# Stick-breaking rows of 512 keys and 16 meta keys: two score matmuls of 256 and 272 columns in place of 512 and 16

## The chip, the cores and the metric

One core of one Trainium2 chip runs the whole kernel. The metric is the device time of one execution in microseconds (us), as the median of several runs.

## The reference

One decoder layer on 2048 tokens of width 1024, with 16 learned meta tokens ahead of them. The input is normalised, projected by one wide matrix, and goes through two attention branches that are gated, projected and added back. The part that matters here is the stick-breaking branch, 8 heads of width 64:

```
z = einsum(q[block], k[:end]) * d ** -0.5          # scores of 128 queries against all keys before them
log_beta = log_sigmoid(z)
log_1m   = where(mask, log_beta - z, 0)            # log(1 - sigmoid(z))
suffix   = sum of log_1m over the keys between this one and the query
w        = where(mask, exp(log_beta + suffix), 0)
out      = w @ v[:end]
```

Each query block of 128 sees every earlier key, and last of all the 16 meta keys. The weight of a key is a difference of two running products of sigmoid(-z), so a scan along the keys gives it.

## The kernel before

TensorE does everything in full precision as pairs of fp32r tiles: a value is split into a high part and a low part, and a product of two values is three matmuls (lines L403, L404 and L405 in the projections, a group of 24 matmuls of 512 columns for each 128 output columns and 512 tokens). The order of TensorE's instructions is written out by hand: `weave` takes a group of three projection matmuls from a main stream and then as much of a side stream as its share of time allows. A scheduler orders the other engines.

The tokens are kept in reverse, so that the scan runs from the query's own block back to the oldest keys, and the meta keys stand at the end of the key list. The sequence is done in two halves (token groups 2 and 3 of 512 tokens first, then groups 0 and 1). In each half the stick-breaking attention, `stick`, is the side stream and the projections of the gates are the main stream. Its steps are rows (head h, group g, key group n, query block j): `row` multiplies 128 queries with up to 512 keys into the PSUM tile `ps_z` (two matmuls, one for each arrangement of the split queries, since the 128 partitions hold the high and the low part of 64 dimensions), ScalarE writes sigmoid(-z) to the SBUF tile `row`, GpSimd sets the masked corner to one in the first key group (`affine_select`), and VectorE scans the row; it starts from the last element of the row before. Five steps later (`LT`) `turn` transposes the scanned blocks on TensorE into `ps_t`, splits them into `wth` and `wtl`, and `values` multiplies them with the differences of the values into `ps_o`. `turn_meta` does the same for the 16 meta columns, through the PSUM tile `ps_zm`.

PSUM has two buffers of one bank for each of `g`, `z` and `t`, and one for `zm` and `o`. A bank holds 512 fp32 columns. Of the rows, only the one with j = 0 in the last key group of a head and token group has 512 keys and the 16 meta keys too: 528 columns, which is more than a bank (`own` in the code). There are 8 heads times 4 token groups = 32 such rows, 16 in each half. Their 16 meta columns go to `ps_zm` by two matmuls of their own (L843), and a second ScalarE instruction reads them (L847). The rows with j = 1, 2 and 3 of that key group have 400, 272 and 144 columns, meta keys included, in one bank. In the first half the step that holds a row of 528 columns for group 2 also holds `turn_meta` for group 3, so that the one buffer of `ps_zm` is wanted again some three matmuls later; in the second half these are eight steps apart.

Of the kernel before, what the change touches and what calls it, by code (L numbers as in the profile page):

```python
# [10 lines left out]
AF = mybir.ActivationFunctionType  # L11
# [9 lines left out]
NM = 16  # L21
# [23 lines left out]
def tile_kernel(ctx, tc, x, xt, meta, metat, gain, w_in, w_sb, w_sw, w_out, sinks, fgain,  # L45
# [6 lines left out]
    V, A, G, T = nc.vector, nc.scalar, nc.gpsimd, nc.tensor  # L52

    def DMA(dst, src):
        nc.sync.dma_start(*(t.bitcast(F32) if t.dtype == F32R else t for t in (dst, src)))
# [6 lines left out]
    def ps(tag):  # L62
        return pp.tile([P, 512], F32, tag=tag, name="ps_" + tag, bufs={"g": 2, "z": 2, "zm": 1, "t": 2, "o": 1}[tag])
# [716 lines left out]
    def stick(groups, bp, sums_of={}):  # L780
        kt, vc = {}, {}
        rows_of = {}
        for g in groups:
            w = wm[g % 2]
# [5 lines left out]
        def load_kv(h, g):  # L790

            p, a = divmod(h, 2)
            r = slice(64 * a, 64 * a + 64)
            if h not in kt:
                kt[h] = bp.tile([P, (4 - groups[0]) * GT + NM], F32R, tag="k", name="kt", bufs=2)
            for c in range(g, 4):
                if (h, c) in vc:
                    continue
                c0 = (c - groups[0]) * GT
                cs = slice(c0, c0 + GT + (NM if c == 3 else 0))  # L800
                DMA(kt[h][0:64, cs], kd[p][c][0][r])
                DMA(kt[h][64:128, cs], kd[p][c][1][r])
                v = vc[h, c] = bp.tile([P, 4, P], F32R, tag="v", name="vc", bufs=5)
                DMA(v, vd[p][c][a])

        def load_q(h, g):
            p, a = divmod(h, 2)
            r = slice(64 * a, 64 * a + 64)
            q1 = bp.tile([P, GT], F32R, tag="q1", name="q1", bufs=2)
            q2 = bp.tile([P, GT], F32R, tag="q2", name="q2", bufs=2)  # L810
            for t in range(2):
                DMA(q1[64 * t:64 * t + 64], qd[p][g][t][r])
                DMA(q2[64 * t:64 * t + 64], qd[p][g][1 - t][r])
            return q1, q2
# [3 lines left out]
        def row(h, g, n, j):  # L818

            if n == j == 0:  # L820
                load_kv(h, g)
                state[h, g] = {"q": load_q(h, g), "last": {}}
                n1 = len(state) - 1
                for g1, ssq in list(sums_of.items())[n1 // 8:n1 // 8 + 1]:
                    i, f = divmod(n1 % 8, 2)
                    t = bp.tile([P, GT], F32, tag="q2", name="xq", bufs=2)
                    DMA(t, x[g1 * GT + i * P:g1 * GT + (i + 1) * P, f * GT:(f + 1) * GT])
                    A.activation(t, t, AF.Square, accum_out=ssq[:, f, i:i + 1])
            st = state[h, g]
            last = st["last"]  # L830
            b0 = 4 * (g + n) + j
            nb = min(4, NB - b0)
            end = b0 + nb == NB
            w = nb * P + (NM if end and nb < 4 else 0)
            k0 = (b0 - 4 * groups[0]) * P
            own = end and nb == 4
            z = ps("z")
            zm = ps("zm") if own else None
            for t, qt in enumerate(st["q"]):
                lq = qt[:, j * P:(j + 1) * P]  # L840
                T.matmul(z[:, :w], lhsT=lq, rhs=kt[h][:, k0:k0 + w], start=t == 0, stop=t == 1)  # L841
                if own:
                    T.matmul(zm[:, :NM], lhsT=lq, rhs=kt[h][:, k0 + w:k0 + w + NM], start=t == 0, stop=t == 1)  # L843
            r = bp.tile([P, RW], F32, tag="row", name="row", bufs=12)
            A.activation(r[:, :w], z[:, :w], AF.Sigmoid, scale=-1.0)  # L845
            if own:
                A.activation(r[:, w:w + NM], zm[:, :NM], AF.Sigmoid, scale=-1.0)  # L847
                w += NM
            if n == 0:
                G.affine_select(out=r[:, :P], in_=r[:, :P], pattern=[[1, P]], compare_op=ALU.is_ge,  # L850
                                fill=1.0, base=-1, channel_multiplier=-1)
            V.tensor_tensor_scan(r[:, :w], r[:, :w], r[:, :w], last[j] if n else 1.0, op0=ALU.mult, op1=ALU.min)  # L852
            last[j] = r[:, w - 1:w]
            rows_of[h, g, n, j] = r
# [46 lines left out]
        for s in range(n + LT + 3):  # L901
            if s < n:
                row(*steps[s])
                yield 0.45
            t = s - LT
            if 0 <= t < n:
                if sum(steps[t][1:3]) == steps[t][3] == 3:
                    turn_meta(*steps[t][:2])
                    turned.append(s)
                    yield 0.43  # L910
                turn(*steps[t])
                turned.append(s)
                yield 0.43
            while av_todo and turned[0] < s - 1:
                del turned[0]
                yield values()
# [170 lines left out]
    for half, groups in enumerate(halves):  # L1087
# [40 lines left out]
        with tc.tile_pool(name=f"sb{half}", bufs=1, side="left") as bp:  # L1128
# [9 lines left out]
            if half == 0:  # L1138
                t, u = (bp.tile([P, GT], F32, tag="wh", name="sum", bufs=3)[:, :8] for _ in range(2))
# [77 lines left out]
```

## Time and profile before

| | |
|---|---|
| time, median of 3 runs | 2168.7 us (2168.49 to 2170.37) |
| the profiled execution: its time, its span | 2172.68 us, 2171.0 us |
| TensorE busy (matmuls) | 2139.1 us, 99% of the span |
| VectorE, ScalarE, GpSimd busy | 1358.0, 1007.2, 372.5 us |
| granted TensorE clock | 0.998 |
| L841, matmuls into `ps_z` | 640, 185.0 us busy |
| L843, matmuls into `ps_zm`, 16 columns | 64, 11.0 us busy |
| L845 and L847, ScalarE sigmoid from `ps_z` and from `ps_zm` | 320 and 32, 171.7 and 5.7 us busy |

PE is TensorE's matmul side and PEld its loading of stationary operands, which runs beside the matmuls. DVE is VectorE, ACT ScalarE, POOL GpSimd, SP the queue that issues all DMAs. The ends of matmuls are modelled by the profiler and overlap the next one's start, so that what a matmul costs is read from start to start in the timeline: 0.23 us for 512 columns, though each is shown as 0.39 us long. A number in brackets at a row's end is idle time ahead of the instruction, and the arrow names what released it.

### The profile page before, as it was taken

What the parts mean: (1) busy time and instruction counts of PE and PEld (TensorE: products, weight loads), DVE (VectorE), ACT (ScalarE), POOL (GpSimd) and SP (SyncE); (2) the same over time, 40 slices, a digit from 0 to 9 for tenths busy, and PEclk for the clock granted to TensorE, in tenths of its full rate; (3) what the DMA queues carried; (4) which work ended last, traced back from release to release, by engine and by line L of the source; (5) the groups of instructions that cost most, each with busy time, mean ns of one, the idle gap of its engine ahead of it and who ended that gap; (6) DMA issues with size and microseconds to landing.
All of it is one profiled execution on the core that took longest, in us unless ns stands there. A gap on an engine that the chain in (4) does not pass through costs nothing. (4 is left out here: it accounts for less than half of the span.)

```text
span 2171.0 us, 30232 instructions
## 1 busy us (share of the span) xinstructions
PE 2139.1 (99%) x10614; PEld 1766.3 (81%) x10614; DVE 1358.0 (63%) x2117; ACT 1007.2 (46%) x2328; POOL 372.5 (17%) x486
## 2 busy tenths in 40 slices
PE   8899999999999999999999999999999999999998
PEld 6678888888888888888887888888888888787887
DVE  7787876465555443767746888787775446454453
ACT  6576775344444434777743555555553201221121
POOL 2233343323222300222310000000000232000000
PEclk9999999999999999999999999999999999999999
DMA  9755455755555464444356433333322985468432
GB/s 330 259 182 195 158 189 186 256 194 201 192 180 178 145 212 155 158 160 147 136 170 184 122 112 115 108 98 118 118 88 92 352 310 191 161 226 274 163 108 88
DMA packets 174648, 380.41 MB, mean 175 GB/s; under 512 B 22912, under 2 KB 41088, under 8 KB 174496
## 3 DMA queue, kind: packets, MB, share of 16 engines
q1 hardware_dynamic: 174496, 378.48, 52.0%
q8 instruction: 84, 1.38, 0.3%
q14 instruction: 68, 0.56, 0.1%
HBM read 237.35 MB, written 140.98 MB: 174 GB/s over the span
## 5 line engine op out<-in xcount | busy, mean ns | idle before, releaser
L403 PE MATMUL ps_g<-xh,wh 128*128 128x512 f32 x1544 | 638.3, 413 | 7.2 <-ACT xh L939 6.8
L405 PE MATMUL ps_g<-xh,wl 128*128 128x512 f32 x1544 | 607.7, 394 | 0.6 <-DVE wl L108 0.6
L404 PE MATMUL ps_g<-xl,wh 128*128 128x512 f32 x1544 | 607.8, 394 | 0.0
L852 DVE TENSOR_TENSOR_SCAN row<-row 128x512 f32<-128x512 f32 (+2 forms) x320 | 371.1, 1162 | 168.2 <-POOL row L850 96.7
L405 PEld LDWEIGHTS ps_g<-xh,wl 128*128 128x128 f32 x1544 | 290.9, 188 | 66.4 <-DVE wl L108 1.1
L403 PEld LDWEIGHTS ps_g<-xh,wh 128*128 128x128 f32 x1544 | 292.0, 189 | 54.5 <-ACT xh L939 6.8
L404 PEld LDWEIGHTS ps_g<-xl,wh 128*128 128x128 f32 x1544 | 292.5, 189 | 44.1 <-DVE xl L940 1.3
L845 ACT ACTIVATE row<-ps_z 128x512 f32<-128x512 f32 (+1 forms) x320 | 171.7, 537 | 252.8 <-PE ps_z L841 209.8
L112 DVE SCALAR_TENSOR_TENSOR wtl<-ps_t,wth 128x512 fp32r<-128x512 f32 (+1 forms) x320 | 189.9, 593 | 47.5 <-ACT wth L111 46.0
L111 ACT ACTIVATE wth<-ps_t 128x512 fp32r<-128x512 f32 (+1 forms) x320 | 170.2, 532 | 92.3 <-PE ps_t L863 90.8
L841 PE MATMUL ps_z<-kt,q 128*128 128x512 f32 (+3 forms) x640 | 185.0, 369 | 0.3 <-ACT row L845 0.3
L863 PE MATMUL ps_t<-ident,row 128*128 128x128 f32 x1088 | 171.6, 273 | 1.2 <-DVE row L852 1.2
L863 PEld LDWEIGHTS ps_t<-ident,row 128*128 128x128 f32 x1088 | 135.9, 140 | 37.3 <-DVE row L852 1.7
L850 POOL TENSOR_SCALAR_AFFINE_SELECT row<-row 128x128 f32<-128x128 f32 x128 | 44.8, 351 | 620.0 <-ACT row L845 552.6
L841 PEld LDWEIGHTS ps_z<-kt,q 128*128 128x128 f32 x640 | 118.7, 188 | 26.4 <-ACT row L845 0.8
L889 PE MATMUL ps_o<-wth,vc 128*128 128x512 f32 (+1 forms) x320 | 125.7, 393 | 1.3 <-DVE tmp L894 1.1
L107 POOL TENSOR_SCALAR wh<-raw 128x1024 fp32r<-128x1024 f32 (+1 forms) x63 | 66.9, 1063 | 327.9 <-PE ps_g L404 213.8
L560 ACT ACTIVATE tmp<-ps_g 128x512 f32<-128x512 f32 x112 | 67.0, 598 | 118.6 <-PE ps_g L405 112.6
L889 PE MATMUL ps_o<-wtl,vc 128*128 128x512 f32 (+1 forms) x320 | 116.8, 365 | 0.0
L706 ACT ACTIVATE sc<-sc,nm 128x129 f32<-128x129 f32 x256 | 100.0, 393 | 35.8 <-DVE nm L704 35.1
L108 POOL TENSOR_TENSOR wl<-raw,wh 128x1024 fp32r<-128x1024 f32 (+1 forms) x43 | 95.7, 2226 | 3.1
L621 POOL TENSOR_TENSOR tmp<-tmp 128x512 f32<-128x512 f32 (+1 forms) x37 | 48.7, 1315 | 203.6 <-DVE tmp L620 158.3
(306 smaller groups left out, 3399.3 us busy)
## 6 DMA issues: line engine op xcount, KB each, us to landing
wh<-h_in_w_in SPq DMA_DIRECT2D x66, 512.0 KB, 3.8
wl<-l_in_w_in SPq DMA_DIRECT2D x66, 512.0 KB, 4.8
raw<-in_w_in SPq DMA_DIRECT2D x50, 512.0 KB, 6.0
h_in_w_in<-wh SPq DMA_DIRECT2D x50, 512.0 KB, 3.6
l_in_w_in<-wl SPq DMA_DIRECT2D x50, 512.0 KB, 2.9
q<-qd SPq DMA_DIRECT2D x128, 128.0 KB, 2.9
vc<-vd SPq DMA_DIRECT2D x48, 256.0 KB, 3.1
kd<-tmp SPq DMA_DIRECT2D x32, 256.0 KB, 4.3
```

The lines of the kernel that those rows point to most:

```text
L108: (V if vsplit[0] else G).tensor_tensor(l, src, f32(h), op=ALU.subtract)
L111: A.activation(h, acc, AF.Copy, scale=scale)
L112: V.scalar_tensor_tensor(l, acc, scale, f32(h), op0=ALU.mult, op1=ALU.subtract)
L403: T.matmul(acc, lhsT=wh[:, k, :], rhs=xh[g][:, k, :], start=k == 0, stop=False)
L404: T.matmul(acc, lhsT=wh[:, k, :], rhs=xl[g][:, k, :], start=False, stop=False)
L405: T.matmul(acc, lhsT=wl[:, k, :], rhs=xh[g][:, k, :], start=False, stop=k == KT - 1)
L706: A.activation(sc[:, hh, :], sc[:, hh, :], AF.Exp, bias=nm[:, hh:hh + 1], accum_out=den[:, hh:hh + 1])
L841: T.matmul(z[:, :w], lhsT=lq, rhs=kt[h][:, k0:k0 + w], start=t == 0, stop=t == 1)
L845: A.activation(r[:, :w], z[:, :w], AF.Sigmoid, scale=-1.0)
L852: V.tensor_tensor_scan(r[:, :w], r[:, :w], r[:, :w], last[j] if n else 1.0, op0=ALU.mult, op1=ALU.min)
L863: T.transpose(tr[:, j * P:(j + 1) * P], rows_of[h, g, n - (j > i), j][:, k0:k0 + P], ident)
L889: T.matmul(o[:, :n], lhsT=v, rhs=r, start=first and r is wh, stop=last and r is wl)
```

## The change

A row of 528 columns is cut into 256 and 272 columns, the first into `ps_z`, the rest with the meta keys into `ps_zm`, and ScalarE reads the two tiles in this order. All other rows stay as they are, and `row` in SBUF has the same layout.

```diff
             own = end and nb == 4
             z = ps("z")
             zm = ps("zm") if own else None
+            parts = [(z, 0, w // 2), (zm, w // 2, w + NM)] if own else [(z, 0, w)]
+            w = parts[-1][2]
             for t, qt in enumerate(st["q"]):
                 lq = qt[:, j * P:(j + 1) * P]
-                T.matmul(z[:, :w], lhsT=lq, rhs=kt[h][:, k0:k0 + w], start=t == 0, stop=t == 1)
-                if own:
-                    T.matmul(zm[:, :NM], lhsT=lq, rhs=kt[h][:, k0 + w:k0 + w + NM], start=t == 0, stop=t == 1)
+                for acc, a, b in parts:
+                    T.matmul(acc[:, :b - a], lhsT=lq, rhs=kt[h][:, k0 + a:k0 + b], start=t == 0, stop=t == 1)
             r = bp.tile([P, RW], F32, tag="row", name="row", bufs=12)
-            A.activation(r[:, :w], z[:, :w], AF.Sigmoid, scale=-1.0)
-            if own:
-                A.activation(r[:, w:w + NM], zm[:, :NM], AF.Sigmoid, scale=-1.0)
-                w += NM
+            for acc, a, b in parts:
+                A.activation(r[:, a:b], acc[:, :b - a], AF.Sigmoid, scale=-1.0)
```

The line numbers behind it move: the matmuls of all rows are on L844 after the change, their ScalarE reads on L847, and what stood on L850 to L894 stands one line earlier.

TensorE's order keeps its length and its neighbours; only the four matmuls of such a row differ. This is a row of the first half with what follows up to `turn_meta`, where `q_4668` and `q_4669` are the two arrangements of the split queries. Before:

```order
L841 MATMUL ps_z<-kt,q_4668 128x512
L843 MATMUL ps_zm<-kt,q_4668 128x16
L841 MATMUL ps_z<-kt,q_4669 128x512
L843 MATMUL ps_zm<-kt,q_4669 128x16
L403 MATMUL ps_g<-xh,wh 128x512
L404 MATMUL ps_g<-xl,wh 128x512
L405 MATMUL ps_g<-xh,wl 128x512
L403 MATMUL ps_g<-xh,wh 128x512
L404 MATMUL ps_g<-xl,wh 128x512
L405 MATMUL ps_g<-xh,wl 128x512
L874 MATMUL ps_zm<-ident,row 16x128 x4
```

After:

```order
L844 MATMUL ps_z<-kt,q_4668 128x256
L844 MATMUL ps_zm<-kt,q_4668 128x272
L844 MATMUL ps_z<-kt,q_4669 128x256
L844 MATMUL ps_zm<-kt,q_4669 128x272
L403 MATMUL ps_g<-xh,wh 128x512
L404 MATMUL ps_g<-xl,wh 128x512
L405 MATMUL ps_g<-xh,wl 128x512
L403 MATMUL ps_g<-xh,wh 128x512
L404 MATMUL ps_g<-xl,wh 128x512
L405 MATMUL ps_g<-xh,wl 128x512
L873 MATMUL ps_zm<-ident,row 16x128 x4
```

Nothing moved here but the columns. Of the 32 rows 23 are followed by a projection matmul (L403), as here, and 9, all in the second half, by transposes (L863).

On the SP queue the scheduler's order differs in two places, both in the first half. At the first, before, where `raw` is a weight tile as it comes from memory, `q` the split queries and `xq` a tile of the input (`zs`, `zw` take results to memory):

```order
L55 DMA l_in_w_in_4989<-wl 128x1024
L55 DMA raw<-in_w_in 128x1024
L55 DMA xq<-in_x 128x512
L55 DMA q_4918<-qd_3_81 64x512 x2
L55 DMA q_4919<-qd_3_81 64x512
L55 DMA zw_2_144<-tmp 128x512
```

After:

```order
L55 DMA l_in_w_in_4989<-wl 128x1024
L55 DMA q_4918<-qd_3_81 64x512
L55 DMA xq<-in_x 128x512
L55 DMA q_4918<-qd_3_81 64x512
L55 DMA raw<-in_w_in 128x1024
L55 DMA q_4919<-qd_3_81 64x512 x2
L55 DMA zw_2_144<-tmp 128x512
```

The load of the weights stands behind two loads of queries and one of the input. At the second place it stands behind one store. On VectorE the scan of a row of 528 columns has moved ahead of one or two other instructions at two places, on GpSimd one `affine_select` ahead of one split, on ScalarE one square of the input ahead of two others.

## The prediction

> **What bounds the kernel.** I read first the busy times on the profile's page, then the busy time by stage, then the waits of TensorE, and at last the timeline around the rows that change.
>
> ```profile
> PE 2139.1 (99%) x10614; PEld 1766.3 (81%) x10614; DVE 1358.0 (63%) x2117; ACT 1007.2 (46%) x2328; POOL 372.5 (17%) x486
> ```
>
> The stage view cuts the span at the two stretches of stick-breaking, 404 to 740 us and 1165 to 1665 us. Its columns are length, then PE, PEld, DVE, ACT and POOL busy, granted clock, DMA share and GB/s.
>
> ```profile
> 404.00:740.00 336.00, 336.00 (x1714) 276.73 (x1713) 188.21 (x235) 140.62 (x305) 94.79 (x107) 1.00 0.56 184
> ...
> 1165.00:1665.00 500.00, 498.56 (x2689) 413.98 (x2690) 403.50 (x492) 269.94 (x526) 17.55 (x60) 1.00 0.34 105
> ```
>
> In both stretches PE is never idle for more than a moment: 0 of 336 us and 1.4 of 500 us. ACT has half its time free, DVE is the next engine with 403.50 of 500 us. So in these stages the end is set by TensorE's own list, and time taken off that list comes off the whole, unless another engine then arrives late. The waits say how near the others are; the numbers are us in total, how often, and the longest.
>
> ```profile
> PE ps_t L863 <- DVE row L852: 1.2, 2, 0.8
> PE ps_z L841 <- ACT row L845: 0.3, 1, 0.3
> PEld ps_zm L874 <- ACT row L847: 2.7, 7, 0.4
> ```
>
> The scan that is the heaviest DVE group holds PE up twice, the sigmoid once. The third row is a wait of the weight side for the ACT read of the meta columns, seven times; I come back to it.
>
> **The change: the matmuls.** A busy PE is made of steps from start to start. This is one of the 32 rows, in the first half, with its ACT reads:
>
> ```profile
> 679.63 0.39 PE L405 MATMUL ps_g<-xh,wl 128*128 128x512 f32 x1
> 679.86 0.39 PE L841 MATMUL ps_z<-kt,q 128*128 128x512 f32 x1
> 679.87 0.19 PEld L843 LDWEIGHTS ps_zm<-kt,q 128*128 128x128 f32 x1
> 680.09 0.17 PE L843 MATMUL ps_zm<-kt,q 128*128 128x16 f32 x1
> 680.12 0.48 PE L841 MATMUL ps_z<-kt,q 128*128 128x512 f32 x1
> 680.44 0.17 PE L843 MATMUL ps_zm<-kt,q 128*128 128x16 f32 x1
> 680.46 0.48 PE L403 MATMUL ps_g<-xh,wh 128*128 128x512 f32 x1
> 680.63 0.60 ACT L845 ACTIVATE row<-ps_z 128x512 f32<-128x512 f32 x1 [2.75 <-PE ps_zm L843]
> 680.78 0.40 PE L404 MATMUL ps_g<-xl,wh 128*128 128x512 f32 x1
> 681.02 0.40 PE L405 MATMUL ps_g<-xh,wl 128*128 128x512 f32 x1
> 681.13 0.18 ACT L847 ACTIVATE row<-ps_zm 128x16 f32<-128x16 f32 x1
> 681.36 0.60 PE L874 MATMUL ps_zm<-ident,row 128*16 128x128 f32 x4
> ```
>
> A 512-column step takes 0.23 us (679.63 to 679.86). The first 512 of the row takes that too, the 16 columns take 0.03 (680.09 to 680.12). But the matmul behind them takes 0.32 (680.12 to 680.44), and so does the projection matmul behind the second (680.46 to 680.78). So a matmul of 16 columns costs 0.03 + 0.09 = 0.12 us: the weights of the next one have nothing to load behind. The four matmuls and this aftermath take 0.60 + 0.09 = 0.69 us.
>
> After the change no matmul is shorter than 256 columns. Steps of 256 columns stand in the trace in the products with the values, and 272 columns in the row with j = 2 (x2 merges its two matmuls):
>
> ```profile
> 438.03 0.28 PE L889 MATMUL ps_o<-wth,vc 128*128 128x256 f32 x1
> 438.15 0.28 PE L889 MATMUL ps_o<-wtl,vc 128*128 128x256 f32 x1
> 438.27 0.39 PE L403 MATMUL ps_g<-xh,wh 128*128 128x512 f32 x1
> 438.96 0.41 PE L841 MATMUL ps_z<-kt,q 128*128 128x272 f32 x2
> 439.22 0.39 PE L403 MATMUL ps_g<-xh,wh 128*128 128x512 f32 x1
> 439.44 0.39 PE L404 MATMUL ps_g<-xl,wh 128*128 128x512 f32 x1
> ```
>
> Two of 256 take 0.24 us, two of 272 take 0.26, and the 512 behind them its plain 0.22, so nothing is left over for the next. The new row costs 0.24 + 0.26 = 0.50 us. The columns are the same 528, so by columns alone it would be 2 x 528 / 512 x 0.23 = 0.47 us; I take 0.50, from the rows with these very shapes. Each row gains 0.69 - 0.50 = 0.19 us where a projection matmul follows, 23 times.
>
> The Trainium skill (TensorE: Matmul & The Clock Gate, LDWEIGHTS) puts a weight load at its columns over 1.2 GHz, by which an estimate for 128 is 107 ns, and a warm matmul of 256 columns at 262 cycles of 2.4 GHz, 109 ns (Back-to-back issue gap). By that the load would still just hide under 256 columns, and the trace's steps agree: 0.12 us behind a matmul too short to hide anything, 0.12 us for 256.
>
> In nine rows transposes follow. This is one, and behind it the same transposes after a matmul pair that hides the load:
>
> ```profile
> 1647.17 0.39 PE L841 MATMUL ps_z<-kt,q 128*128 128x512 f32 x1
> 1647.75 0.17 PE L843 MATMUL ps_zm<-kt,q 128*128 128x16 f32 x1
> 1647.78 0.64 PE L863 MATMUL ps_t<-ident,row 128*128 128x128 f32 x4
> 1648.17 0.48 PE L403 MATMUL ps_g<-xh,wh 128*128 128x512 f32 x1
> ...
> 1652.05 0.41 PE L841 MATMUL ps_z<-kt,q 128*128 128x272 f32 x2
> 1652.30 0.60 PE L863 MATMUL ps_t<-ident,row 128*128 128x128 f32 x4
> 1652.65 0.47 PE L889 MATMUL ps_o<-wth,vc 128*128 128x512 f32 x1
> ```
>
> The row takes 0.61 us (1647.17 to 1647.78), and its transposes 0.39 in place of 0.35: 0.04 more. That makes 0.65 - 0.50 = 0.15 us of gain, which I use for all nine, also for the five with a single transpose behind them.
>
> Sum: 23 x 0.19 + 9 x 0.15 = 4.4 + 1.3 = 5.7 us off TensorE's list, 3.0 us of it in the first half and 2.7 in the second.
>
> **The change: ScalarE and the wait behind it.** The rows of the groups, with mean ns of one:
>
> ```profile
> L845 ACT ACTIVATE row<-ps_z 128x512 f32<-128x512 f32 x224 | 133.6, 597 | 183.5 <-PE ps_z L841 140.7 <-PE ps_zm L843 42.3
> L847 ACT ACTIVATE row<-ps_zm 128x16 f32<-128x16 f32 x32 | 5.7, 178 | 0.0
> L845 ACT ACTIVATE row<-ps_z 128x272 f32<-128x272 f32 x32 | 12.7, 397 | 25.2 <-PE ps_z L841 25.2
> L111 ACT ACTIVATE wth<-ps_t 128x256 fp32r<-128x256 f32 x32 | 12.2, 383 | 7.4 <-PE ps_t L863 7.4
> ```
>
> 597 + 178 = 775 ns becomes 383 + 397 = 780 ns (256 columns from another ACT read of PSUM): nothing, and ACT has the room. In the timeline the second read starts 0.50 us after the first, 0.10 before its end, so the pair lasts 0.68 us before and after. What counts is when `ps_zm` is free. In the first half `turn_meta` writes it next: its transposes start at 681.36, though the 512 ahead of them started at 681.02 and was over by 0.23 later, at 681.25. PE loses 0.11 us there, waiting for ACT's read to end at 681.31. Before, that read ends 1.45 us behind the row's start at 679.86. After, the second 256-column matmul starts 0.25 into the row, is shown with 0.28 us, and ACT starts some 0.03 later, at 0.56; its two reads end at 1.24, 0.21 us sooner than before. PE comes there 0.19 sooner, so the wait of 0.11 stays and the gain is kept. If instead ACT's first read starts only when the last of the four matmuls is done, 0.12 us later, the 8 such places (group 2 of each head) keep 0.12 us less each: bounds 0 and 8 x 0.12 = 1.0 us. I take 0, since ACT waits for the tile that it reads.
>
> VectorE scans 528 columns as before and can start 0.2 us sooner. The scan that moved ahead of a gate's multiplication on DVE may hold a `ps_g` bank about 1.3 us longer; PE returns to that bank only after the other's 24 matmuls of 0.23 us, 5.5 us, which cover it. On the SP queue the load of `raw` goes behind two loads of queries, some 5 us. These are its issue, the POOL split of the weights that it feeds, and the page's row of such loads (KB each, median us to landing):
>
> ```profile
> 407.65 0.42 SPq L55 DMA_DIRECT2D raw<-in_w_in  x1
> 420.81 1.05 POOL L107 TENSOR_SCALAR wh<-raw 128x1024 fp32r<-128x1024 f32 x1 [4.35 <-PE ps_g L404]
> raw<-in_w_in SPq DMA_DIRECT2D x50, 512.0 KB, 6.0
> ```
>
> The split waits for PE to free a weight buffer, not for the load, 13 us behind its issue; with 6 us to landing, some 7 us of slack cover the move. If that cover went, the split would be late by a microsecond or two, but the tile that it makes is used only when two older weight tiles of 48 matmuls each have been used up, 22 us.
>
> Sum: 5.7 us. The profiled execution's span becomes 2171.0 - 5.7 = 2165.3 us, its time 2172.68 - 5.7 = 2167.0. That execution lies 4 us above the median of the runs; from the median 2168.7 I get 2163.0 us, 0.26% less.
>
> **The rivals.** First, that VectorE takes the place of TensorE in the second half. For it speaks 403.50 of 500 us busy there; it scans in order, and a stage with its row's chain tight gives nothing back. Against it: PE waited for the scan twice, 1.2 us in all. If it were so, only the first half's 3.0 us would stay, less up to 1.0 for `ps_zm`: 2165.7 to 2166.7 us.
>
> Second, that the weight loads are not hidden by 256 columns. This is the one that would make it slower. A load is shown as 0.19 us, longer than a step of 0.12. If each of the four matmuls took that, a row would cost 0.76 us in place of 0.69 or 0.65: 23 x 0.07 + 9 x 0.11 = 2.6 us more, 2171.3 us. It turns into a loss at a mean step of (23 x 0.69 + 9 x 0.65) / 32 / 4 = 0.17 us. Against it stand the 256-column pairs at 0.12 a step. What those rows don't show is four such loads in a row with `q` as the stationary tile.
>
> Third, that no load hides at all, so that four loads stand on both sides, the columns are the same, and nothing changes: 2168.7 us. The Trainium skill has a rule that would make it so: loads overlap running matmuls only when their row groups differ (TensorE: Matmul & The Clock Gate, The mechanism), and here all use the whole array. The trace disagrees: a load of 0.19 us runs from 679.87 inside a 512 that started at 679.86, and the next starts 0.23 later.
>
> **How the numbers follow.** The forecast, all of the gain with at most the 1.0 us of `ps_zm` taken off, has 0.70: 2162.0 (columns alone, 0.03 less in each of 32 rows: 1.0 us more gain) to 2164.0. VectorE's share has 0.18, loads half or wholly uncovered 0.05, nothing hidden or another cancelling 0.07. About 0.2%, 4.3 us, is what a measurement of this kernel can tell from no change, and 5.7 us is not far above it. Faster by more than that takes the forecast and a few cases beside it, 0.72; within it 0.25, among them nearly all of the second rival, whose 2.6 us are not 4.3; slower 0.03. The range runs from 2161.5, below the columns alone by the runs' own spread, to 2166.9, which takes in VectorE's case and leaves out the two with no gain.
>
> **What would show it.** The row's four steps should stand at 0.12, 0.13, 0.12 and 0.13 us with a plain 0.23 behind them, PE's starts from the first row to the last of a stretch closer by 3.0 and 2.7 us, the stretches' PE still full, and the wait of L873 for ACT's read no longer than before. A third of a microsecond for a pair, or 0.3 for the L403 behind it, would show loads uncovered. New PE waits for scans in the second half would show VectorE.

## The result and the profile after

The change takes 2162.76 us (median of 7 runs, 2161.79 to 2165.21) against 2168.7 us before (median of 7, 2166.31 to 2170.37): a ratio of 0.9971, with a 95% interval of 0.9962 to 0.9981. That is 5.9 us, against 5.7 forecast; the interval goes from 4.1 to 8.2 us, so that the times alone would agree with 5 or 7 as well. The ratios of the experiments below are against 26 further runs of before, median 2168.24 us, of which one slow run (6615.79 us) is left out.

The busy times on the page:

```profile
PE 2131.1 (99%) x10614; PEld 1762.0 (82%) x10614; DVE 1355.6 (63%) x2117; ACT 1008.0 (47%) x2328; POOL 374.6 (17%) x486
```

The row that the prediction showed from 679.86 on, in the timeline after:

```profile
675.49 0.28 PE L844 MATMUL ps_z<-kt,q 128*128 128x256 f32 x1
...
675.61 0.29 PE L844 MATMUL ps_zm<-kt,q 128*128 128x272 f32 x1
...
675.74 0.28 PE L844 MATMUL ps_z<-kt,q 128*128 128x256 f32 x1
...
675.85 0.29 PE L844 MATMUL ps_zm<-kt,q 128*128 128x272 f32 x1
...
675.98 0.40 PE L403 MATMUL ps_g<-xh,wh 128*128 128x512 f32 x1
...
676.05 0.39 ACT L847 ACTIVATE row<-ps_z 128x256 f32<-128x256 f32 x1 [2.54 <-PE ps_z L844]
676.21 0.39 PE L404 MATMUL ps_g<-xl,wh 128*128 128x512 f32 x1
...
676.33 0.39 ACT L847 ACTIVATE row<-ps_zm 128x272 f32<-128x272 f32 x1
676.44 0.40 PE L405 MATMUL ps_g<-xh,wl 128*128 128x512 f32 x1
...
676.78 0.60 PE L873 MATMUL ps_zm<-ident,row 128*16 128x128 f32 x4
```

Read from start to start: 0.12, 0.13, 0.11, 0.13, and then 0.23 for L403, with nothing left over. The row takes 0.49 us where it took 0.60 and 0.09 of aftermath. Over the 23 rows with a projection matmul behind them the mean is 0.488 us after and 0.687 before.

With transposes behind it, the row that the prediction showed from 1647.17 on:

```profile
1639.84 0.28 PE L844 MATMUL ps_z<-kt,q 128*128 128x256 f32 x1
...
1640.33 0.60 PE L862 MATMUL ps_t<-ident,row 128*128 128x128 f32 x4
1640.69 0.48 PE L403 MATMUL ps_g<-xh,wh 128*128 128x512 f32 x1
```

0.49 us and 0.36 for the transposes, in place of 0.61 and 0.39.

How much of this reaches the whole is best read from the rows of the matmuls into `ps_z`, which tell when the first and the last of the 640 start. Before, and then after (min, median and max ns, then the two starts):

```profile
L841 PE MATMUL ps_z<-kt,q x640: 227/392/506, 404.4 to 1654.0; 128*128 128x512 f32 x128, 128*128 128x272 f32 x32
```

```profile
L844 PE MATMUL ps_z<-kt,q x640: 227/392/506, 402.7 to 1646.5; 128*128 128x512 f32 x96, 128*128 128x256 f32 x32, 128*128 128x272 f32 x32
```

From the first row to the last 1249.6 us before and 1243.8 after: 5.8 us, all of the change. By halves of the program, the first goes from 330.2 us (404.4 to 734.6) to 327.0 (402.7 to 729.7), the second from 495.6 (1158.4 to 1654.0) to 492.9 (1153.6 to 1646.5): 3.2 and 2.7 us less, where the prediction had 3.0 and 2.7. The spans of the two profiled executions differ by more, 2171.0 against 2160.2 us. The other 5.0 us lie ahead of this stretch (404.4 against 402.7) and behind it (517.0 against 513.7), where no instruction changed; in the profiles of the experiments below the stretch starts anywhere from 401.8 to 405.9. So one span against another says little here, and one stretch against another a lot.

ScalarE's two reads, and the waits that the prediction named (weight side, then matmul side):

```profile
L847 ACT ACTIVATE row<-ps_zm 128x272 f32<-128x272 f32 x32 | 12.5, 392 | 0.0
L847 ACT ACTIVATE row<-ps_z 128x256 f32<-128x256 f32 x32 | 12.3, 384 | 39.9 <-PE ps_z L844 39.9
```

```profile
PEld ps_zm L873 <- ACT row L847: 2.8, 7, 0.5
```

```profile
PE ps_t L862 <- DVE row L851: 1.2, 2, 0.8
```

384 + 392 ns stand for 597 + 178. The wait for `ps_zm` is about as it was (2.7 us, 7 times before), the one for the scan the same.

### The profile page after: what moved, and what is told of

It reads as the page before. It is cut to its first block, busy times and chain, and to the rows that moved or that the text cites. A ratio compares the mean times of both kernels' runs of the same rounds, so it can differ in the third digit from the quotient of the medians.

```text
span 2160.2 us, 30234 instructions
## 1 busy us (share of the span) xinstructions
PE 2131.1 (99%) x10614; PEld 1762.0 (82%) x10614; DVE 1355.6 (63%) x2117; ACT 1008.0 (47%) x2328; POOL 374.6 (17%) x486
## 4 chain that ended last, share of the span: by engine, by line
PE 90%; DMA 3%; ACT 2%; DVE 2%; issue 1%; SPq 1%; POOL 0%; ACTq 0%; DVEq 0%; POOLq 0%
PE ps_g L403 15%; PE ps_g L404 15%; PE ps_g L405 15%; PE ps_o L888 6%; PE ps_z L844 5%; PE ps_t L862 5%; PE ps_o L744 3%; PE ps_z L698 3%; PE ps_g L224 1%; PE ps_g L225 1%; PE ps_g L223 1%; PE ps_z L223 1%; PE ps_z L225 1%; PE ps_z L224 1%; PE ps_t L727 1%; PE ps_t L225 1%
## 5 line engine op out<-in xcount | busy, mean ns | idle before, releaser
L403 PE MATMUL ps_g<-xh,wh 128*128 128x512 f32 x1544 | 635.6, 412 | 7.1 <-ACT xh L938 6.6
L403 PEld LDWEIGHTS ps_g<-xh,wh 128*128 128x128 f32 x1544 | 291.7, 189 | 53.5 <-ACT xh L938 6.9
L847 ACT ACTIVATE row<-ps_z 128x512 f32<-128x512 f32 (+2 forms) x320 | 165.1, 516 | 250.8 <-PE ps_z L844 250.2
L844 PE MATMUL ps_z<-kt,q 128*128 128x512 f32 (+4 forms) x640 | 178.2, 354 | 0.3 <-ACT row L847 0.3
L844 PEld LDWEIGHTS ps_z<-kt,q 128*128 128x128 f32 x640 | 118.7, 188 | 25.0 <-ACT row L847 0.8
```

Of the source, the lines that this page charges most:

```text
L403: T.matmul(acc, lhsT=wh[:, k, :], rhs=xh[g][:, k, :], start=k == 0, stop=False)
L844: T.matmul(acc[:, :b - a], lhsT=lq, rhs=kt[h][:, k0 + a:k0 + b], start=t == 0, stop=t == 1)
L847: A.activation(r[:, a:b], acc[:, :b - a], AF.Sigmoid, scale=-1.0)
```

## The experiments

The theory: a matmul on a busy TensorE costs the longer of its own stream and the load of the next one's weights. A 16-column matmul streams in next to nothing, so most of the load behind it is uncovered, and 256 columns are about where this ends. The trace books the lost time on the matmul behind: that one is shown to start only 0.03 us after the short one, and its own step to the next is then 0.09 too long. The rivals: ScalarE gets its tile sooner; the scheduler's other order; the mere number or balance of pieces. Each code difference below is against the change, and ` ...` marks lines left out.

In all of them the stretch from the first to the last matmul into the scores is the finest measure, since it leaves out the parts of the program that vary for themselves.

**Order alone.** The cut of before, with both matmuls of 512 first and both of 16 behind them:

```diff
-            parts = [(z, 0, w // 2), (zm, w // 2, w + NM)] if own else [(z, 0, w)]
+            parts = [(z, 0, w), (zm, w, w + NM)] if own else [(z, 0, w)]
 ...
-            for t, qt in enumerate(st["q"]):
-                lq = qt[:, j * P:(j + 1) * P]
-                for acc, a, b in parts:
+            for acc, a, b in parts:
+                for t, qt in enumerate(st["q"]):
 ...
```

> The cut stays 512 and 16; only the order of the row's four matmuls is new: both of 512, then both of 16. Theory (a 16-column matmul hides no weight load, so each one makes its successor about 0.09 us late): still two short matmuls, so a row still costs about 0.69 us where a projection follows (0.46 for the two of 512, then 0.11 and 0.03 + 0.09), and the time is that of before within 1 us, 2168 to 2169.5. The second short matmul should start 0.11 us behind the first. Rival A (the gain comes from ScalarE getting its tile sooner): here ScalarE can start the 512 columns about 0.14 us sooner, so part of the gain, 2165 to 2167. Rival B (the gain is the scheduler's other order): no forecast, but a time as of the change would speak for it.

Measured 2167.29 us, a ratio to before of 0.9997 (0.9988 to 1.0006): no change that can be told. Its first row in the timeline, its stretch, and the wait for `ps_zm`:

```profile
402.76 0.63 PE L843 MATMUL ps_z<-kt,q 128*128 128x512 f32 x2
403.23 0.28 PE L843 MATMUL ps_zm<-kt,q 128*128 128x16 f32 x2
403.37 0.48 PE L403 MATMUL ps_g<-xh,wh 128*128 128x512 f32 x1
403.68 0.40 PE L404 MATMUL ps_g<-xl,wh 128*128 128x512 f32 x1
```

```profile
L843 PE MATMUL ps_z<-kt,q x640: 228/392/498, 402.8 to 1651.7; 128*128 128x512 f32 x128, 128*128 128x272 f32 x32
```

```profile
PEld ps_zm L873 <- ACT row L847: 2.0, 7, 0.3
```

0.47 for the two of 512, 0.14 for the two of 16, 0.31 for the L403 behind: 0.61 + 0.08, as before. Two details of the expectation missed: the second short matmul starts 0.03 us behind the first, and only L403 0.11 behind that, so that the sum of the two is as expected; and the time is 0.7 below the expected range, which was set from a median of before of 2168.7 and not 2168.24. The stretch is 1248.9 us, 0.7 less than before, and the gain is in the first half (402.8 to 732.1, 329.3 us, 0.9 less). There TensorE no longer stands still for `ps_zm`: before, in seven places, the meta transposes started 0.34 to 0.35 us behind the 512 columns ahead of them, 0.8 us lost in all; here they start 0.23 to 0.26 behind. The weight side still shows a wait of 2.0 us, but under cover of the running matmul. So ScalarE's earlier start is worth some 0.8 us, and rival A falls as the source of 5.8. On rival B this run says nothing: in the two stretches the other engines and the SP queue have the order of before.

**Twice the short matmuls.** The 16 columns as two pieces of 8, with the two matmuls of each piece next to each other:

```diff
-            parts = [(z, 0, w // 2), (zm, w // 2, w + NM)] if own else [(z, 0, w)]
+            parts = [(z, 0, w), (zm, w, w + NM)] if own else [(z, 0, w)]
 ...
+            cuts = [(z[:, :w - NM], 0), (zm[:, :8], w - NM), (zm[:, 8:NM], w - 8)] if own else [(z[:, :w], 0)]
+            for acc, a in cuts:
+                n1 = acc.shape[1]
+                for t, qt in enumerate(st["q"]):
+                    T.matmul(acc, lhsT=qt[:, j * P:(j + 1) * P], rhs=kt[h][:, k0 + a:k0 + a + n1],
+                             start=t == 0, stop=t == 1)
```

> The 16 meta columns go as two pieces of 8, so each of the 32 rows has four short matmuls in place of two; the columns and ScalarE's reads are as before. Theory (each short matmul costs one uncovered weight load, 0.11 us): 2 x 0.11 x 32 = 7.2 us more than before, about 2176 (2174.5 to 2177), steps of 0.11 from short to short. Rival (short matmuls cost their columns and a small floor of 0.03 us each; the 0.32 behind them has another cause, such as the switch of bank): 2 x 0.03 x 32 = 1.9 us more, 2170.6.

Measured 2173.47 us, a ratio of 1.0026 (1.0016 to 1.0036): 3.5 to 7.8 us slower.

```profile
402.76 0.63 PE L845 MATMUL ps_z<-kt,q 128*128 128x512 f32 x2
403.22 0.50 PE L845 MATMUL ps_zm<-kt,q 128*128 128x8 f32 x4
403.58 0.49 PE L403 MATMUL ps_g<-xh,wh 128*128 128x512 f32 x1
403.91 0.40 PE L404 MATMUL ps_g<-xl,wh 128*128 128x512 f32 x1
```

```profile
L845 PE MATMUL ps_z<-kt,q x640: 227/392/507, 402.8 to 1658.9; 128*128 128x512 f32 x128, 128*128 128x272 f32 x32
```

Four matmuls of 8 columns take 0.36 us and the next one 0.33: 0.46 + 0.36 + 0.10 = 0.92 us a row, 0.23 more than before. The price of a short matmul is 0.11 us, and 8 columns cost what 16 cost; nor is it the switch of bank, since all four write the same tile. The rival's 1.9 us lie below the interval. The stretch is 1256.1 us, 6.5 more than before, 0.7 short of the 7.2 expected, and the time fell below the expected range with it. The wait for `ps_zm`, 2.7 us before, no longer stands in the list of waits: TensorE now comes too late to wait in the first half, which gives back about 0.8: that half grew by 2.8 us (402.8 to 735.8, 333.0), the second by 3.7, with 16 such rows in each. The expectation had left that out.

**The cut at 384.**

```diff
+            parts = [(z, 0, 384), (zm, 384, w + NM)] if own else [(z, 0, w)]
```

> The same change with the cut at 384: 384 and 144 columns. Theory (a matmul costs the longer of its stream, 0.45 ns a column, and the next weight load, 0.112 us): 144 columns stream in 0.065, so 0.047 stay uncovered: a row costs 2 x (0.173 + 0.112) = 0.57 us against 0.69 and 0.49, so 0.12 of gain where a projection follows and some 0.07 where transposes do: 23 x 0.12 + 9 x 0.07 = 3.4 us, about 2165.3 (2164.3 to 2166.3). Rival (any second piece that is not tiny does, or the balance is for ScalarE's sake): as the change, 2162.8.

Measured 2164.43 us, a ratio of 0.9983 (0.9974 to 0.9992).

```profile
403.15 0.34 PE L844 MATMUL ps_z<-kt,q 128*128 128x384 f32 x1
403.32 0.23 PE L844 MATMUL ps_zm<-kt,q 128*128 128x144 f32 x1
403.39 0.39 PE L844 MATMUL ps_z<-kt,q 128*128 128x384 f32 x1
403.62 0.23 PE L844 MATMUL ps_zm<-kt,q 128*128 128x144 f32 x1
403.68 0.44 PE L403 MATMUL ps_g<-xh,wh 128*128 128x512 f32 x1
403.96 0.39 PE L404 MATMUL ps_g<-xl,wh 128*128 128x512 f32 x1
```

```profile
L844 PE MATMUL ps_z<-kt,q x640: 227/392/506, 403.1 to 1649.5; 128*128 128x512 f32 x96, 128*128 128x384 f32 x32, 128*128 128x272 f32 x32
```

The first 384 takes 0.17, the second, which stands behind 144 columns, 0.23, some 0.05 too long, and L403 takes 0.28. This row costs 0.53 + 0.05 = 0.58 us, the mean row 0.57, and the stretch is 1246.4 us, 3.2 less than before against 3.4 expected. So a second piece that is merely not tiny is not enough. By the time alone the rival of 2162.8 lies just inside the interval (0.9974 x 2168.24 = 2162.6); the steps and the stretch decide.

**The two tiles swapped.**

```diff
+            parts = [(zm, 0, w // 2), (z, w // 2, w + NM)] if own else [(z, 0, w)]
```

> The change with the two tiles swapped: the first 256 columns go to ps_zm, the 272 with the meta keys to ps_z. ps_zm is then read first by ScalarE and free 0.4 us sooner. Theory: TensorE's steps as in the change, and the wait of the meta transposes for ScalarE (7 times 0.1 us in the first half) goes: 0.8 us less than the change, about 2162.0, too little to tell by the time, but the wait should be gone from the list of waits. Rival (this wait is not ScalarE's read of ps_zm but the scan or the transposes' own order): the wait stays as it is.

Measured 2161.16 us, a ratio to before of 0.9967 (0.9956 to 0.9979). The same row as above, the wait, and the first and last starts:

```profile
675.17 0.28 PE L844 MATMUL ps_zm<-kt,q 128*128 128x256 f32 x1
...
675.74 0.38 ACT L847 ACTIVATE row<-ps_zm 128x256 f32<-128x256 f32 x1 [2.54 <-PE ps_zm L844]
...
676.36 0.60 PE L873 MATMUL ps_zm<-ident,row 128*16 128x128 f32 x4
```

```profile
PEld ps_zm L873 <- ACT row L847: 0.2, 1, 0.2
```

```profile
L844 PE MATMUL ps_z<-kt,q x640: 227/392/506, 403.1 to 1645.8; 128*128 128x512 f32 x96, 128*128 128x272 f32 x64
...
L844 PE MATMUL ps_zm<-kt,q x64: 278/282/284, 403.0 to 1639.3; 128*128 128x256 f32 x64
```

ScalarE has read `ps_zm` by 676.12, and the meta transposes start 1.19 us behind the row's start, in place of 1.29 in the change. Of 2.8 us of waits 0.2 are left (a wait of the weight side that is 0.4 long holds the matmuls up by only 0.1), and the stretch, from 403.0 to 1645.8, is 1242.8 us, 1.0 less than the change's, nearly all of it in the first half (403.0 to 729.1, 326.1 us against 327.0). This version has the lowest median of all that were run several times; its lead over the change is smaller than the times can tell.

**The cut at 192 and at 128**, one run each, to see where the load stops being covered:

```diff
+            parts = [(z, 0, 192), (zm, 192, w + NM)] if own else [(z, 0, w)]
```

```diff
+            parts = [(z, 0, 128), (zm, 128, w + NM)] if own else [(z, 0, w)]
```

> The change with the cut at 192: 192 and 336 columns, one look for the steps. Theory (a step is the longer of the stream, 0.45 ns a column, and a weight load of 0.112 us): 192 columns stream in 0.087, so their step and what it leaves to the next come to 0.112, 336 columns 0.152: a row costs 2 x 0.264 = 0.53 us, with nothing left over for the matmul behind, since the last piece is long. Rival (a fixed cost for any extra matmul, whatever its length, as between 144 and 256 columns alike): 0.57 as with 384 and 144.

> The change with the cut at 128: 128 and 400 columns, one look for the steps. Theory: 128 columns stream in 0.058, cost 0.112 with what they leave to the next; 400 columns 0.180: a row costs 2 x 0.292 = 0.58 us. The short piece stands first, so that the cost shows inside the row and the projection matmul behind keeps its 0.23. Rival as with 192 columns.

Single times were 2160.47 us with 192 and 2169.28 with 128, which says little, as the spans above showed. The steps, with 192 and then with 128:

```profile
401.75 0.25 PE L844 MATMUL ps_z<-kt,q 128*128 128x192 f32 x1
401.84 0.34 PE L844 MATMUL ps_zm<-kt,q 128*128 128x336 f32 x1
402.02 0.25 PE L844 MATMUL ps_z<-kt,q 128*128 128x192 f32 x1
...
402.28 0.39 PE L403 MATMUL ps_g<-xh,wh 128*128 128x512 f32 x1
```

```profile
405.94 0.22 PE L844 MATMUL ps_z<-kt,q 128*128 128x128 f32 x1
406.00 0.40 PE L844 MATMUL ps_zm<-kt,q 128*128 128x400 f32 x1
406.24 0.22 PE L844 MATMUL ps_z<-kt,q 128*128 128x128 f32 x1
...
406.53 0.39 PE L403 MATMUL ps_g<-xh,wh 128*128 128x512 f32 x1
```

The pair of 192 and 336 takes 0.27 us (401.75 to 402.02), the pair of 128 and 400 takes 0.30 (405.94 to 406.24), and the whole rows 0.53 and 0.59: as the theory had them, 0.53 and 0.58. The rival with one price for every cut, 0.57, has 192 wrong. Their stretches:

```profile
L844 PE MATMUL ps_z<-kt,q x640: 227/392/506, 401.8 to 1646.4; 128*128 128x512 f32 x96, 128*128 128x192 f32 x32, 128*128 128x272 f32 x32
```

```profile
L844 PE MATMUL ps_z<-kt,q x640: 220/392/506, 405.9 to 1652.6; 128*128 128x512 f32 x96, 128*128 128x128 f32 x32, 128*128 128x272 f32 x32
```

1244.6 us for 192 and 1246.7 for 128. With the others, in order of the shortest piece:

| shortest piece, columns | cost of a row with L403 behind, us | stretch against before, us |
|---|---|---|
| 8 and 8 | 0.91 | +6.5 |
| 16 (before) | 0.69 | 0 |
| 16, other order | 0.69 | -0.7 |
| 128 | 0.58 | -2.9 |
| 144 | 0.57 | -3.2 |
| 192 | 0.53 | -5.0 |
| 256 (the change) | 0.49 | -5.8 |
| 256, tiles swapped | 0.49 | -6.8 |

The cost column is a mean over the 23 rows; the stretches come from starts to 0.1 us, so that a difference can be off by 0.1. With the tiles swapped a row costs the same, so it does not matter which tile takes which piece. How balanced the pieces are changes here together with the shortest piece, but the overlong steps stand on TensorE itself, in rows where it waits for no other engine. The scheduler's order, rival B, is not the source: the cut at 384 has the change's order on the SP queue throughout, the cut at 128 has its order on VectorE and GpSimd, and they gain only 3.2 and 2.9 us, about what their rows give.

One rival would give the same table: a floor of 0.11 us under any matmul that has a load of its own, however short the load. Rows that are the same in all these kernels speak against it; here as before has them. The projections of the meta tokens (L414) also stream 128 columns, but load only 48 columns of weights each:

```profile
33.28 0.22 PE L414 MATMUL ps_zm<-wh,mx 128*48 128x128 f32 x1
...
34.24 0.45 PE L403 MATMUL ps_o<-uh,wh 128*128 128x512 f32 x1
34.54 0.40 PE L404 MATMUL ps_o<-ul,wh 128*128 128x512 f32 x1
```

Sixteen of them take 0.96 us (33.28 to 34.24), 0.06 each, which is their stream of 128 x 0.45 ns. Only the last has a full load of 128 columns behind it, and the L403 there takes 0.30 in place of 0.23. With full loads behind them, 128 columns cost 0.11 in the cut at 128. So the price goes with the length of the load. It is not a rule for all that TensorE does: the four transposes of L874 in the prediction's row load 16 columns each and still take 0.11 us each (681.36 to 681.72, and 0.09 more in the step of the L403 behind); why, no run here shows.

## Why the prediction was right

**The bound.** It said that time off TensorE's list comes off the whole. The stretch shrank by 5.8 us where the list shrank by 5.7 as worked out, and the runs by 5.9. No other engine took its place: the VectorE rival would have left the 3.0 us of the first half, but the second half gave its 2.7 too, and the waits for the scan are the same 1.2 us. That the runs' 5.9 came so near to 5.7 is in part luck, given their interval; the stretch's 5.8 is not.

**The matmuls.** 0.50 us was taken for the new row and 0.49 measured; 0.69 for the old one, also the mean measured. For the nine rows with transposes 0.15 was taken: 0.61 + 0.39 became 0.49 + 0.36, which is 0.15. That the old cost was an uncovered weight load was an inference from two late starts in one row; doubling the short matmuls has shown the price, 0.11 for each (the prediction's 0.12 was a reading from rounded starts), the cuts at 128, 144 and 192 have shown that it goes as the columns grow, and the L414 rows that it goes with the load. The Trainium skill's figure for a load of 128 columns, 107 ns by its rule of columns over 1.2 GHz (TensorE: Matmul & The Clock Gate, LDWEIGHTS), is close to the 0.11 us steps of the 8-column matmuls. The Trainium skill's rule that the third rival drew on, that loads overlap matmuls only with other row groups (TensorE: Matmul & The Clock Gate, The mechanism, which elsewhere also lets a load go ahead into a background weight buffer), is not what this trace shows: then no cut would have differed from another in its loads.

**The wait for `ps_zm`.** The prediction held that ScalarE's first read starts when its own tile is done, 0.56 us into the row, and that the wait of 0.11 stays. It starts at 676.05, 0.56 behind 675.49, and the transposes start at 676.78, 0.11 behind the end of the projection's last step (676.44 + 0.23). The bound of 1.0 us was not needed. The swap has shown that this wait was ScalarE's read and could be had as well, for 1.0 us in the stretch.

**The moved load.** It was put at some 5 us later, with 7 of slack. The SP queue's rows and the split that waits for it, after:

```profile
405.61 0.32 SPq L55 DMA_DIRECT2D l_in_w_in<-wl  x1
...
407.83 0.58 SPq L55 DMA_DIRECT2D raw<-in_w_in  x1
```

```profile
418.74 1.05 POOL L107 TENSOR_SCALAR wh<-raw 128x1024 fp32r<-128x1024 f32 x1 [4.42 <-PE ps_g L404]
```

The load is issued 2.2 us behind the store ahead of the queries (405.61), where it had been 0.4 behind it, so it lost under 2 us, and the split waits for TensorE as it did. The size was off, the conclusion not.

The chance of 0.25 for no change that can be told was due to the size: 5.7 us is 0.26%. The interval leaves 0.19% as the least gain, so that this remains near the limit of what the times alone can show. The trace's stretch tells it far more finely.

## What to carry to other kernels

On a TensorE that is never idle, look for matmuls that are shorter than the weight load behind them: each costs the load, here 0.11 us for 8 columns as for 16, and the cost stands in the step of the matmul behind it, which is too long. Where the columns don't fit one bank, cut them so that both pieces stay above that length (an estimate of 250 columns here, where the stream's 0.45 ns a column reaches 0.11 us; in the runs 192 fell short and 256 did not) in place of filling one bank and leaving a remainder. And let the tile whose buffer is wanted first be the one that is read first.

## What was not expected

A piece of 8 columns costs as much as one of 16, and the shown durations hide it: the profile gives a 16-column matmul 0.17 us and a 512 one 0.39, where they cost 0.11 and 0.23. And the profiled spans of kernels that differ in a few matmuls, 2158.7 to 2172.1 us, vary by several microseconds outside the changed stretch, so that a single execution put the cut at 128 columns, which saves 2.9 us in its stretch, above the run of before beside it (2169.28 against 2167.95 us).
